# Putting the second layer's modulation products behind a later weight split, up to the first output projection

## The chip, the cores and the metric

The kernel runs on one core of a Trainium2 chip. The metric is the device time of one execution in microseconds (us). The engines are named as in the profile: PE (TensorE matmul), PEld (its weight loads), DVE (VectorE), ACT (ScalarE), POOL (GpSimd) and SP (SyncE, whose queue carries almost all of the loads).

## The reference, cut to what matters

Two residual layers of width 2048 work on 256 positions; a context of 256 positions feeds the first layer alone. Each layer begins with a modulation and ends with a gated residual and a layer norm:

```python
m = jax.nn.silu(cond) @ w_ada[i] + b_ada[i]      # 3 * 2048 outputs
sh, sc, gt = jnp.split(m, 3, axis=-1)
u = x * (1.0 + sc) + sh
y = mixer(u)          # layer 0: gated linear attention and a short convolution; layer 1: pooling
x = layer_norm(alpha * x + gt * y, ln_g[i], ln_b[i])
```

All is float32. `w_ada` is 2 x 2048 x 6144, so a third of it (one of `sh`, `sc`, `gt` of one layer) is 2048 x 2048, 16.8 MB. The two projections of layer 0 are `w_in_e` (2048 x 8224) and `w_out_e` (2048 x 2048), those of layer 1 `w_in_o` (2048 x 4096) and `w_out_o` (2048 x 2048).

## The kernel before

**Weight units.** Every large weight comes in units of 512 rows (four tiles of 128) by 512 columns, 1 MB each, by one DMA on SP's queue into a pool of four buffers (`raw`, L96). Each float32 unit is split into a rounded part and a remainder: ACT casts `wh` (L154), DVE subtracts to `wl` (L155), two instructions of each a unit. The parts lie in pools of four tiles each, which is two units. A product is three matmuls of 512 columns (`mm3`, L192 to L194). The list `specs` fixes the order of the units. `w_next` takes the next one; before that `w_ahead` loads up to two units further and splits one further. Below, units are counted along `specs` from 0.

**Modulation units.** The products of one row of activations with `w_ada` for layer 1's `sc` and `sh` and for both layers' `gt` are not made on PE. `ada_unit` (L505) loads 512 rows by 512 columns, 1 MB, into the same four `raw` buffers on the same queue, and `ada_accum` (L552) adds four tiles to an accumulator on DVE (L558 for the first, L560 for the rest). Four such units make a block of 512 columns. A block ends with small matmuls over the partitions: `adaS` (L581) for `sc` and `sh`, `gtb` (L547) for `gt`. Three generators run in the order `sc` of layer 1 (`c`), `gt` of layer 0 (`g`), `sh` of layer 1 (`h`), four blocks each, so 48 units. A fourth one makes layer 1's `gt` during layer 1.

**Pacing.** After each unit of a projection `tick` (L635) adds a credit and `pump_ada` (L497) takes that many steps of the generators. A step is one unit, or one end of a block. The credit of a tick is 3 during the six V units (`ADA_V`), 0.4 for the 16 units of q and of the first gate (`ADA_X`), 0.8 for the 32 units of the convolution branch (`ADA_C`), 1 during the output projection of layer 0 (`ADA_O`).

**The output projection of layer 0** (`ln_blocks`, L1102, called in L1196) takes 16 units, 76 to 91 along `specs`, in column blocks 0, 1, 2 and 3. Units 88 to 91 are block 3. Its matmuls run by row tile: row tile 0 with all four units, then row tile 1 with the same four. Ahead of block 3, `before()` calls `cols_ab` (L1166), which runs `pump_ada(1000)`: all that is left of the generators. Then come `A1` and `B1`, and `B1` (L1171) needs all of `sh`. `to_u1` (L1173) normalizes row tile 0 while PE works on row tile 1; it scales by `A1` and `B1` and gives the input of layer 1.

**Order on the engines.** The program text gives each instruction a place in a priority order; the framework orders each engine's instructions by that order and by when its own estimate finds them ready, and each engine then runs its list in order. Splits are raised by 300 places (`SPLIT_PRIO`). Loads keep their place in the text.

Of the kernel before, what the change touches and what calls it, by code (L numbers as in the profile page):

```python
# [9 lines left out]
F32 = mybir.dt.float32  # L10
# [3 lines left out]
ALU = mybir.AluOpType  # L14
# [48 lines left out]
def kernel(  # L63
# [24 lines left out]
    nc = tc.nc  # L88
    names = {}

    def nm(s):
        names[s] = names.get(s, 0) + 1
        return f"{s}_{names[s]}"
# [17 lines left out]
    def const(shape, dt, name):  # L111
        return cpool.tile(shape, dt, tag=name, name=name)
# [4 lines left out]
    def mp(shape, name="mp"):  # L117
        return mpp.tile(shape, F32, tag="mp", name=nm(name))
# [26 lines left out]
    def split_unit(r, nk, wide=False):  # L145
        parts = []
        for j in range(0, nk, 2):
            w = min(2, nk - j)
            if wide:
                h, l = slot([P, w, 512], F32R, "swh"), slot([P, w, 512], F32R, "swl")  # L150
            else:
                h = whp.tile([P, w, 512], F32R, tag="wh", name=nm("wh"))
                l = wlp.tile([P, w, 512], F32R, tag="wl", name=nm("wl"))
            nc.scalar.copy(h, r[:, j : j + w, :])  # L154
            nc.vector.tensor_tensor(out=l, in0=r[:, j : j + w, :], in1=h.bitcast(F32), op=ALU.subtract)  # L155
            for i in range(w):
                parts.append((h[:, i, :], l[:, i, :]))
        return parts
# [5 lines left out]
    wst = {"l": 0, "s": 0, "u": 0}  # L164
    wraws, wparts = {}, {}

    def w_ahead(nl, ns):
        top = len(specs)
        while wst["s"] < min(top, wst["u"] + ns):
            w_load(wst["s"] + 1)  # L170
            i = wst["s"]
            with prio(-SPLIT_PRIO if n0_done[0] else -SPLIT_PRIO0):
                wparts[i] = split_unit(wraws.pop(i), specs[i][2], i in wide)
            wst["s"] = i + 1
        w_load(min(top, wst["u"] + nl))

    def w_load(n):
        while wst["l"] < n:
            i = wst["l"]
            wraws[i] = load_unit(*specs[i])  # L180
            wst["l"] = i + 1
# [149 lines left out]
    k0 = 0  # L331
# [164 lines left out]

    def pump_ada(n):  # L497
        while n > 0 and ada_bg:
            try:
                next(ada_bg[0])  # L500
                n -= 1
            except StopIteration:
                ada_bg.pop(0)

    def ada_unit(layer, k0, n0):  # L505

        if not ADA_SLOT:
            r = load_unit(w_ada[layer], k0, 4, n0)
            return [r[:, j, :] for j in range(4)]
        q = {"s": nc.sync, "g": nc.gpsimd}[ADA_SLOT]  # L510
        parts = []
        for k in (k0, k0 + 2):
            r = slot([P, 2, 512], F32, "araw")
            q.dma_start(r, w_ada[layer][k * P : (k + 2) * P, n0 : n0 + 512].rearrange("(k p) n -> p k n", p=P))
            parts += [r[:, 0, :], r[:, 1, :]]
        return parts
# [16 lines left out]
    def ada_rows_gen(layer, dst, engs):  # L533

        for nb in range(4):
            if nb % 2 == 0:
                dst.append(slot([P, 2, 512], F32, "gt"))
            g = dst[nb // 2][:, nb % 2, :]
            n0 = 2 * D + nb * 512
            nc.gpsimd.dma_start(g, b_ada[layer : layer + 1, n0 : n0 + 512].to_broadcast([P, 512]))  # L540
            a = small([P, 512], "aacc1")
            for k0 in range(0, KT, 4):
                ada_accum(ada_unit(layer, k0, n0), k0, a, engs)
                if k0 == KT - 4:
                    yield
                    pb = mp([P, 512], "gtb")
                    nc.tensor.matmul(out=pb, lhsT=ones, rhs=a, start=True, stop=True)  # L547
                    nc.vector.tensor_tensor(out=g, in0=pb, in1=g, op=ALU.add)
                    gt_done.setdefault(id(dst), set()).add(nb)
                yield  # L550

    def ada_accum(r, k0, a, engs):  # L552
        e = engs[(k0 // 4) % len(engs)]
        with prio(ADA_PRIO):
            for j in range(4):
                sc = sil[:, k0 + j, 2:3]
                if k0 + j == 0:
                    e.tensor_scalar(out=a, in0=r[j], scalar1=sc, scalar2=None, op0=ALU.mult)  # L558
                else:
                    e.scalar_tensor_tensor(out=a, in0=r[j], scalar=sc, in1=a, op0=ALU.mult, op1=ALU.add)  # L560

    def ada_cols_gen(layer, n0, dst, bias, one, engs, on_pe=()):

        for nb in range(4):
            ns = slice(4 * nb, 4 * nb + 4)
            if nb in on_pe:
                hold = []
                for _ in ada_acc_gen(layer, n0 + nb * 512, hold):
                    if not hold:
                        yield  # L570
                add_bias(dst[:, ns], to_cols(hold[0], 512)[:, :, 0], bias[:, ns], one)
                yield
                continue
            a = small([P, 512], "aacc1")
            for k0 in range(0, KT, 4):
                ada_accum(ada_unit(layer, k0, n0 + nb * 512), k0, a, engs)
                yield
            yield
            pt = mp([P, 4], "adaS")
            for q in range(4):  # L580
                nc.tensor.matmul(out=pt[:, q : q + 1], lhsT=a[:, q * P : (q + 1) * P], rhs=ones[:, 0:1], start=True, stop=True)  # L581
            add_bias(dst[:, ns], pt, bias[:, ns], one)
# [9 lines left out]
    prev, k0 = None, 0  # L592
# [494 lines left out]
    for i in range(2):  # L1087
        n0 = i * 512
# [13 lines left out]
    def ln_blocks(src, order, getu, res, gt, budget, after, before=None, between=None, halves=False):  # L1102

        rt, accs, seen = {}, {}, {}

        def add(nb, m, cs=slice(0, 512)):
            if nb not in rt:
                rt[nb] = res(nb)
            while ada_bg and not (len(gt) > nb // 2 and nb in gt_done.get(id(gt), ())):
                pump_ada(1)  # L1110
            t = small([P, 512], "arow")[:, cs]
            nc.vector.tensor_tensor(out=t, in0=accs[nb][m + (cs.start > 0)][:, cs], in1=gt[nb // 2][:, nb % 2, cs], op=ALU.mult)
            r = rt[nb][:, m, cs]
            nc.vector.scalar_tensor_tensor(out=r, in0=r, scalar=ALPHA, in1=t, op0=ALU.mult, op1=ALU.add)
            parts = [r] if not (halves and m) or cs != slice(0, 512) else [r[:, 0:256], r[:, 256:512]]
            for v in parts:
                nc.vector.bn_stats(out=cst[m][:, seen_st[m], :], in_=v)
                seen_st[m] += 1

        def done(m, cs, end):  # L1120
            with prio(-LN_PRIO if m else 0):
                add(order[-1][0], m, cs)
                if not end:
                    return
                mv = small([P, 2], "mv")
                nc.vector.bn_aggr(out=mv, in_=cst[m][:, 0 : seen_st[m], :])
                after(m, rt, mv[:, 0:1], mv[:, 1:2])

        seen_st = [0, 0]
        for nb, qs in order[:-1]:  # L1130
            if 1 in qs:
                drain()
            if nb not in accs:
                accs[nb] = [acc_bank("oacc") for _ in range(2)]
                seen[nb] = 0
            gemm(src, nb * 512, qs, range(2), getu, accs[nb], first=seen[nb] == 0, last=seen[nb] + len(qs) == 4, budget=budget)
            seen[nb] += len(qs)
            if seen[nb] == 4:
                for m in range(2):
                    add(nb, m)  # L1140
        if before:
            before()
        nb, qs = order[-1]
        accs[nb] = [acc_bank("oacc") for _ in range(2)]
        gemm_by_tile([(src, nb * 512, qs, accs[nb], True)], getu, done, between=between, halves=halves)
        return rt
# [12 lines left out]
        return r  # L1159

    ada_credit[1] = ADA_O
    A1 = const([P, KT], F32, "A1")
    B1 = const([P, KT], F32, "B1")
    u1h, u1l, ufs, dms = [], [], [], []

    def cols_ab():  # L1166
        ln_exp_tables()
        pump_ada(1000)
        nc.vector.tensor_tensor(out=A1, in0=lngT, in1=scT1, op=ALU.mult)
        nc.vector.tensor_tensor(out=B1, in0=lnbT, in1=scT1, op=ALU.mult)  # L1170
        nc.vector.tensor_tensor(out=B1, in0=B1, in1=shT1, op=ALU.add)  # L1171

    def to_u1(m, rt, mean, var):  # L1173
        rstd = rsqrt_act(var)
        ms = slice(m * P, (m + 1) * P)
        for nb in range(4):
# [10 lines left out]
            for j in range(4):  # L1187
                kt = 4 * nb + j
                if j % 2 or (UF_ACT >> m) & 1:
                    nc.scalar.activation(uf[:, j, :], pt[:, j, :], AF.Identity, bias=B1[:, kt : kt + 1], scale=A1[:, kt : kt + 1])  # L1190
                else:
# [136 lines left out]
    for s in ODD:  # L1328
        g = int(s[1])
        if s == "g0":  # L1330
            accs = [acc_bank("xacc") for _ in range(2)]
            f = gate_evac(0)
# [81 lines left out]
```

## Time and profile before

| | |
|---|---|
| median of 3 runs | 997.5 us (997.06 to 998.74) |
| profiled execution | 1001.09 us |
| its span, first to last instruction | 999.3 us |
| mean granted TensorE clock | 0.983 of full speed |
| busy: PE / DVE / ACT | 959.7 / 801.0 / 469.4 us |
| DMA | 255.44 MB, mean 256 GB/s |

Matmuls overlap in the records, so PE counts as busy where one begins before the last has ended. Where PE is idle, work was late. Of DVE and of the DMA queues only that idle or busy time matters which PE has to wait for.

### The profile page before, as it was taken

The numbers are of one execution on the slowest core, as the hardware profiler recorded it, in microseconds if no ns is written. First come the engines' busy times: TensorE is split into PE (matmuls) and PEld (weight loads), VectorE is DVE, ScalarE is ACT, GpSimd is POOL, SyncE is SP. The second block draws the span as 40 slices with busy tenths as digits, with TensorE's granted clock in tenths as the row PEclk, the third lists the DMA queues.
The fourth block names the chain that finished last, engine by engine and source line by source line (L and its number), as shares of the span: only waits on it lengthen the run. The fifth ranks groups of instructions, "written<-read, shape, count | busy, mean of one in ns | idle before, by whom it ended". The sixth has DMA issues, their size and how long they took to land.

```text
span 999.3 us, 14376 instructions
## 1 busy us (share of the span) xinstructions
PE 959.7 (96%) x5684; PEld 767.0 (77%) x5684; DVE 801.0 (80%) x1143; ACT 469.4 (47%) x643; POOL 24.4 (2%) x56
## 2 busy tenths in 40 slices
PE   7899999999999999999999899999989999989995
PEld 5566766888878877887878788887778778768885
DVE  1456657999996999789999779897979997676676
ACT  2432224265774775245554344346644555444340
POOL 2000000000000000000000000000100001000000
PEclk9899999999999999999999999999999999999998
DMA  9988999577786677857776787994697999775532
GB/s 258 291 268 294 306 330 333 208 244 261 247 289 225 206 254 227 275 194 253 253 253 211 274 300 272 320 327 149 207 349 269 313 334 319 269 280 186 182 114 84
DMA packets 150371, 255.44 MB, mean 256 GB/s; under 512 B 5078, under 2 KB 46720, under 8 KB 150304
## 3 DMA queue, kind: packets, MB, share of 16 engines
q1 hardware_dynamic: 146592, 245.13, 72.8%
q0 software_dynamic: 2896, 8.72, 2.8%
q10 hardware_dynamic: 816, 0.68, 0.3%
q8 instruction: 44, 0.72, 0.3%
q14 instruction: 23, 0.19, 0.1%
HBM read 252.41 MB, written 2.10 MB: 255 GB/s over the span
## 4 chain that ended last, share of the span: by engine, by line
PE 56%; DVE 24%; DMA 14%; issue 3%; ACT 2%; SPq 1%; DVEq 0%; ACTq 0%
DMA raw<-in_w_ada_dram 11%; DVE wl L155 8%; PE oacc L193 6%; PE oacc L192 6%; PE oacc L194 6%; DVE aacc L560 6%; PE xacc L194 6%; PE xacc L192 6%; PE xacc L193 6%; DMA raw<-in_w_in_o_dram 3%; PE kacc L192 2%; PE ada L287 2%; PE kacc L193 2%; PE kacc L194 2%; ACT wh L154 1%
## 5 line engine op out<-in xcount | busy, mean ns | idle before, releaser
L154 ACT CAST wh<-raw 128x1024 fp32r<-128x1024 f32 (+1 forms) x250 | 257.3, 1044 | 256.7 <-PE xacc L194 86.0
L155 DVE TENSOR_TENSOR wl<-raw,wh 128x1024 fp32r<-128x1024 f32 (+1 forms) x250 | 297.8, 1210 | 50.2 <-ACT wh L154 48.3
L560 DVE SCALAR_TENSOR_TENSOR aacc<-raw,sil,aacc 128x512 f32<-128x512 f32 x240 | 178.8, 747 | 31.2 <-DMA raw<-in_w_ada_dram 27.8
L192 PE MATMUL xacc<-wh,uxh 128*128 128x512 f32 x384 | 154.1, 401 | 0.0
L193 PE MATMUL xacc<-wl,uxh 128*128 128x512 f32 x384 | 151.4, 394 | 0.9 <-DVE wl L155 0.9
L194 PE MATMUL xacc<-wh,uxl 128*128 128x512 f32 x384 | 151.6, 395 | 0.0
L193 PEld LDWEIGHTS xacc<-wl,uxh 128*128 128x128 f32 x384 | 72.8, 189 | 17.5 <-DVE wl L155 1.8
L192 PEld LDWEIGHTS xacc<-wh,uxh 128*128 128x128 f32 x384 | 72.8, 190 | 15.6 <-issue 0.5
L194 PEld LDWEIGHTS xacc<-wh,uxl 128*128 128x128 f32 x384 | 72.6, 189 | 15.6 <-issue 0.2
L452 DVE TENSOR_TENSOR knat<-kacc,knat 128x512 f32<-128x512 f32 x64 | 42.9, 685 | 32.1 <-PE kacc L194 31.8
L300 ACT COPY arow<-ada 128x256 f32<-128x256 f32 (+1 forms) x9 | 3.1, 349 | 93.2 <-PE ada L287 93.2
L192 PE MATMUL xacc<-wh,u1h 128*128 128x512 f32 x112 | 45.2, 403 | 0.8 <-ACT u1h L1193 0.8
L192 PE MATMUL oacc<-wh,y1h 128*128 128x512 f32 (+1 forms) x120 | 45.5, 379 | 0.0
L194 PE MATMUL oacc<-wh,y1l 128*128 128x512 f32 (+1 forms) x120 | 45.0, 375 | 0.0
L193 PE MATMUL oacc<-wl,y1h 128*128 128x512 f32 (+1 forms) x120 | 45.0, 375 | 0.0
L193 PE MATMUL xacc<-wl,u1h 128*128 128x512 f32 x112 | 44.6, 398 | 0.4 <-DVE wl L155 0.4
L194 PE MATMUL xacc<-wh,u1l 128*128 128x512 f32 x112 | 44.2, 395 | 0.0
L287 PE MATMUL ada<-raw,sil 128*32 128x256 f32 (+1 forms) x576 | 33.9, 367 | 7.8 <-DMA raw<-in_w_ada_dram 7.7
L287 PEld LDWEIGHTS ada<-raw,sil 128*32 128x32 f32 x576 | 15.7, 110 | 23.7 <-issue 9.4
L1254 PE MATMUL xacc<-wh,dm 128*128 128x512 f32 x64 | 26.2, 410 | 2.7 <-ACT wh L154 2.7
L192 PE MATMUL kacc<-wh,uxh 128*128 128x512 f32 x64 | 26.8, 419 | 0.0
L193 PE MATMUL kacc<-wl,uxh 128*128 128x512 f32 x64 | 26.0, 407 | 0.0
(342 smaller groups left out, 1874.9 us busy)
## 6 DMA issues: line engine op xcount, KB each, us to landing
raw<-in_w_ada_dram SPq DMA_DIRECT2D x96, 1024.0 KB, 6.4
raw<-in_w_in_e_dram SPq DMA_DIRECT2D x54, 1024.0 KB, 5.7
raw<-in_w_in_o_dram SPq DMA_DIRECT2D x32, 1024.0 KB, 7.1
raw<-in_w_out_e_dram SPq DMA_DIRECT2D x16, 1024.0 KB, 6.4
raw<-in_w_out_o_dram SPq DMA_DIRECT2D x16, 1024.0 KB, 5.1
raw<-in_w_in_e_dram SPq DMA_DIRECT2D x18, 512.0 KB, 6.3
raw<-in_w_pool_dram SPq DMA_DIRECT2D x4, 1024.0 KB, 7.7
gt<-in_b_ada_dram POOLq DMA_DIRECT2D x8, 256.0 KB, 3.9
```

The source lines that it names most:

```text
L154: nc.scalar.copy(h, r[:, j : j + w, :])
L155: nc.vector.tensor_tensor(out=l, in0=r[:, j : j + w, :], in1=h.bitcast(F32), op=ALU.subtract)
L192: nc.tensor.matmul(out=acc, lhsT=uh, rhs=wh, start=start, stop=False)
L193: nc.tensor.matmul(out=acc, lhsT=uh, rhs=wl, start=False, stop=False)
L194: nc.tensor.matmul(out=acc, lhsT=ul, rhs=wh, start=False, stop=stop)
L287: ins = nc.tensor.matmul(out=ps[32 * g : 32 * g + 32, :], lhsT=sil[:, kt, 2 - 2 * half : 34 - 2 * half], rhs=r[:, j, :], start=half == 0 a ...
L300: arow_ins.append(nc.scalar.copy(a[:, :nw], ps))
L452: nc.vector.tensor_tensor(out=dst, in0=acc, in1=dst, op=ALU.add)
L560: e.scalar_tensor_tensor(out=a, in0=r[j], scalar=sc, in1=a, op0=ALU.mult, op1=ALU.add)
L1254: nc.tensor.matmul(out=accs[0], lhsT=dh, rhs=wh, start=f, stop=False)
```

## The change

Up to layer 0's output projection, a modulation unit is still loaded at its step, but its four DVE instructions are put off. `put_off` files them with the number of weight units loaded so far. `w_ahead` issues them once it has split the first weight unit that was loaded after them, ordered behind that unit's last subtraction. At most two units are on file: a third pushes the first one out at once. A block's end waits for its products: as long as any are on file, the generator yields, and each such yield is a step that `pump_ada` counts. From the output projection on (`defer[0] = False`) products are issued directly, as before.

```diff
+            wl_ins.append(nc.vector.tensor_tensor(out=l, in0=r[:, j : j + w, :], in1=h.bitcast(F32), op=ALU.subtract))
...
+    def put_off(f):
+        if not defer[0]:
+            f()
+            return
+        while len(pend) >= 2:
+            pend.pop(0)[1]()
+        pend.append((wst["l"], f))
+
+    def pend_all():
+        while pend:
+            pend.pop(0)[1]()
...
             wst["s"] = i + 1
+            while pend and pend[0][0] <= i:
+                with tc.issue_after(wl_ins[-1].ins):
+                    pend.pop(0)[1]()
...
     def pump_ada(n):
         while n > 0 and ada_bg:
+            if n >= 500:
+                pend_all()
...
-                ada_accum(ada_unit(layer, k0, n0), k0, a, engs)
+                put_off(lambda r=ada_unit(layer, k0, n0), k0=k0, a=a: ada_accum(r, k0, a, engs))
                 if k0 == KT - 4:
                     yield
+                    while pend:
+                        yield
...
-                ada_accum(ada_unit(layer, k0, n0 + nb * 512), k0, a, engs)
+                put_off(lambda r=ada_unit(layer, k0, n0 + nb * 512), k0=k0, a=a: ada_accum(r, k0, a, engs))
+                yield
+            while pend:
                 yield
             yield
...
             while ada_bg and not (len(gt) > nb // 2 and nb in gt_done.get(id(gt), ())):
+                pend_all()
                 pump_ada(1)
...
     ada_credit[1] = ADA_O
+    defer[0] = False
+    pend_all()
```

## Rows read from the trace of the kernel before

**Rows 1.** Busy time over the span (page, part 1)

```profile
PE 959.7 (96%) x5684; PEld 767.0 (77%) x5684; DVE 801.0 (80%) x1143; ACT 469.4 (47%) x643; POOL 24.4 (2%) x56
```

**Rows 2.** By stretch: length, busy PE, PEld, DVE, ACT, POOL; clock, DMA share, GB/s

```profile
182.00:274.00 92.00, 92.00 (x432) 76.18 (x431) 85.62 (x136) 53.90 (x82) 0.51 (x5) 1.00 0.69 240
274.00:322.00 48.00, 45.96 (x271) 37.17 (x270) 39.90 (x54) 31.83 (x45) 1.41 (x5) 1.00 0.79 271
322.00:372.00 50.00, 50.00 (x459) 40.18 (x458) 49.98 (x63) 36.51 (x37) 0.00 (x0) 1.00 0.71 232
372.00:466.00 94.00, 92.60 (x683) 75.56 (x682) 81.83 (x117) 46.53 (x64) 1.06 (x2) 1.00 0.71 234
466.00:560.00 94.00, 93.94 (x756) 76.78 (x754) 91.33 (x123) 44.59 (x59) 1.40 (x2) 1.00 0.72 240
560.00:595.00 35.00, 32.04 (x138) 26.19 (x136) 24.30 (x45) 15.67 (x22) 1.50 (x3) 0.90 0.78 278
595.00:646.00 51.00, 51.00 (x242) 42.55 (x241) 46.55 (x63) 21.57 (x24) 0.00 (x0) 1.00 0.87 308
646.00:671.40 25.40, 25.40 (x118) 21.09 (x117) 25.04 (x31) 12.12 (x12) 0.00 (x0) 1.00 0.88 304
```

**Rows 3.** PE's waits from 182 to 600: us in total, times, longest

```profile
PE yT L1000 <- DVE y L992: 3.0, 1, 3.0
...
PE xacc L193 <- DVE wl L155: 0.9, 2, 0.6
```

**Rows 4.** PE and DVE in order of time around 569: start, us, [idle before]

```profile
569.25 0.75 DVE L560 SCALAR_TENSOR_TENSOR aacc<-raw,sil,aacc 128x512 f32<-128x512 f32 x1 [3.35 <-DMA raw<-in_w_ada_dram]
569.92 1.26 DVE L992 SCALAR_TENSOR_TENSOR y<-po,rsy,gs 128x256 f32<-128x256 f32 x3
...
570.55 1.09 PE L1000 MATMUL yT<-ident,y 128*128 128x128 f32 x4 [2.96 <-DVE y L992]
...
571.86 0.63 PE L193 MATMUL xacc<-wl,uxh 128*128 128x512 f32 x1
572.29 0.63 PE L194 MATMUL xacc<-wh,uxl 128*128 128x512 f32 x1
```

**Rows 5.** Line L560 alone from 182 to 274: busy (x instructions), clock, DMA

```profile
182.00:274.00 92.00, 39.43 (x53) 1.00 0.69 240
```

**Rows 6.** SP's waits before a load, over the span

```profile
SPq L140 <- DVE aacc L560: 139.4, 57, 8.7
```

**Rows 7.** SP's loads in order of time, from 645

```profile
645.95 0.37 SPq L140 DMA_DIRECT2D raw<-in_w_ada_dram  x1
646.61 16.39 SPq L140 DMA_DIRECT2D raw<-in_w_out_e_dram  x5
```

**Rows 8.** A stretch of steady loads, columns as in rows 2

```profile
100.00:180.00 80.00, 78.69 (x559) 56.31 (x558) 53.52 (x89) 23.36 (x41) 0.41 (x2) 1.00 0.99 320
```

**Rows 9.** DMA rate in slices of 2 us, 720 to 800

```profile
GB/s 372 326 376 264 288 325 399 386 386 388 378 376 334 368 251 363 406 381 384 351 305 132 369 38 51 287 200 261 300 350 387 295 226 140 394 298 407 373 354 193
```

**Rows 10.** DVE in order of time: one unit's four products in one piece

```profile
623.55 3.11 DVE L560 SCALAR_TENSOR_TENSOR aacc<-raw,sil,aacc 128x512 f32<-128x512 f32 x4
```

**Rows 11.** DVE's groups from 646 to 672: count, busy us, mean ns

```profile
L155 DVE TENSOR_TENSOR wl<-raw,wh 128x1024 fp32r<-128x1024 f32 x8 | 9.6, 1219 | 0.4 <-ACT wh L154 0.4
L560 DVE SCALAR_TENSOR_TENSOR aacc<-raw,sil,aacc 128x512 f32<-128x512 f32 x9 | 6.7, 744 | 0.0
```

**Rows 12.** PE and DVE in order of time, last block of the output projection

```profile
671.54 0.39 PE L192 MATMUL oacc<-swh,yah 128*128 128x512 f32 x1
...
676.98 0.39 PE L192 MATMUL oacc<-wh,ybh 128*128 128x512 f32 x1
...
685.99 0.68 DVE L1194 TENSOR_TENSOR u1l<-uf,u1h 128x512 fp32r<-128x512 f32 x1
...
690.10 0.39 PE L192 MATMUL xacc<-wh,u1h 128*128 128x512 f32 x1
```

**Rows 13.** ACT's half of a split (page, part 5)

```profile
L154 ACT CAST wh<-raw 128x1024 fp32r<-128x1024 f32 (+1 forms) x250 | 257.3, 1044 | 256.7 <-PE xacc L194 86.0
```

More of the change, by code (lines that the diff above doesn't have):

```diff
@@ L154, in split_unit @@
             nc.scalar.copy(h, r[:, j : j + w, :])
-            nc.vector.tensor_tensor(out=l, in0=r[:, j : j + w, :], in1=h.bitcast(F32), op=ALU.subtract)
+            wl_ins.append(nc.vector.tensor_tensor(out=l, in0=r[:, j : j + w, :], in1=h.bitcast(F32), op=ALU.subtract))
             for i in range(w):
@@ L165 @@
     wraws, wparts = {}, {}
+    pend, wl_ins = [], []
+    defer = [True]
+    def put_off(f):
[8 more added lines that the diff above has]
+            pend.pop(0)[1]()
     def w_ahead(nl, ns):
```

## The prediction

> **What bounds the kernel now.** I read the page's first part, then busy time by stretch. PE is busy for 959.7 of 999.3 us [rows 1], and the stretches say where it is not. From 182 to 595, which is V to the end of the convolution branch and so the whole reach of the putting off, idle PE sums to 0 + 2.04 + 0 + 1.40 + 0.06 + 2.96 = 6.5 us; from 595 to 671.4, in the output projection, it is 0 [rows 2]. So PE is the bound. DVE is nearly one too (91.33 of 94 from 466 to 560, 25.04 of 25.4 from 646 to 671.4 [rows 2]), but its work pays only where PE waits for it.
>
> Then PE's waits from 182 to 600. The longest is 3.0 us at 570 for `y`; two for `wl` make 0.9 [rows 3]. The order of time shows the first one's cause: DVE waits 3.35 us, in front of `y`, for the load of a modulation unit [rows 4]. The gap costs more than itself. PE's granted clock over the 35 us from 560 is 0.90 [rows 2], so 0.10 x 35 / 0.5 = 7 us of it ran at the lower level, 1.2 GHz, with matmuls 0.43 us apart [rows 4] where 24 of them from 671.54 to 676.98 are 0.227 apart [rows 12]. That is 7 x (1 - 0.227 / 0.43) = 3.3 us lost.
>
> **Part 1: products behind a later split.** The DVE instructions stay the same, 4 a unit, 3.11 us in one piece [rows 10]; only their place changes. A unit put off after unit u waits for the split of u+3, made two units later, so its load has landed by then and DVE no longer waits for it. Best case: 3.0 for the gap, 3.3 for its clock and 0.9 for the two late `wl`, 7.2 us gained. Against it, a unit on file keeps its buffer longer, and at most two of four are so kept. SP already waits 57 times, 139.4 us in all and at most 8.7, for products to free a buffer [rows 6]. PE feels none of it, as the loads run two units ahead, about 11 us at 24 x 0.227 = 5.4 a unit. I bound the loss at one such wait laid bare, 8.7 us. I take a gain of 5, near the best case because the one large gap has the very cause that is removed.
>
> **Part 2: the steps.** This decides. While a block waits for products on file, the generator yields, and `pump_ada` counts each yield as a step. Steps before the output projection: 6 x 3 + 16 x 0.4 + 32 x 0.8 = 50. Before, a block takes 5 steps (4 units and its end), so 50 steps are 10 blocks, 40 units. The trace agrees for the first stretch: 53 instructions of L560 from 182 to 274, with 4 of L558 14 units of the V stage's 15 [rows 5].
>
> After, in V: tick 1 files units 1 to 3 (the third pushes out the first). Tick 2 files unit 4 and spends two steps waiting, tick 3 all three: unit 4 leaves the file only with the split before tick 4. Tick 4 makes the end and two units of the next block, tick 5 two units and a wait, tick 6 three waits. So V's 18 steps give 8 units, 1 end and 9 waits, where before they gave 15 units and 3 ends. The 16 slow units lose 1 more step and the convolution's 32 lose 2, by the same walk. That is 12 lost, 38 left: 7 blocks and 3 units, 31 units instead of 40.
>
> What does V gain from the 7 units it sheds? Nothing: PE is busy for 92.00 of its 92.00 us [rows 2].
>
> **Part 3: where the 9 units go.** 17 are left for the output projection, where 8 were. Its first 12 ticks make 12 steps: 9 units and 3 ends. The other 8 units go to `pump_ada(1000)` in one piece, right in front of block 3. In text order the loads are then: unit 87, one modulation unit, 88, another, 89, the eight, 90, 91. On SP's queue, in order and through four buffers, 90 is the 14th load counted from 87. Before, 87 is issued at 646.61 and all of 87 to 91 within 16.39 us [rows 7].
>
> A load's price in a steady stretch: 1.049 MB at 320 GB/s and a DMA share of 0.99 [rows 8] is 3.28 us. 14 x 3.28 = 45.9, so unit 90 lands at 692.5. DVE gives about the same: from 646 to 671.4 it works 25.04 us [rows 2], of which products are 6.7 and the split of 91 2.4 [rows 11], so 16 remain; ten units add 10 x 3.11 = 31.1 [rows 10]; 646 + 47.1 = 693.1. With the first cast (1.04 [rows 13]) and subtraction (1.22 [rows 11]) PE can begin unit 90 at 694.8. Before, it began at 671.54 [rows 12].
>
> Row tile 1's share of 88 and 89 (5.4 us) can be pulled into the gap. But row tile 0 must end before `to_u1`: 694.8, unit 91 split 3.28 later at 698.1, its 12 matmuls until 700.8. From that end to layer 1's first input tile took 676.98 to 686.67, 9.7 us [rows 12]. So layer 1 starts at 710.5 instead of 690.10 [rows 12]: 20.4 us late. PE then stood idle for over 10 us; the fall to the lower clock adds between 0 and the 3.3 above, and I take 2. Loss: 22.4.
>
> Bounds of it. Low: each load at the 386 GB/s that several slices reach [rows 9], 2.72 us. Then 90 lands at 684.7, row tile 0 ends at 692.4, layer 1 starts at 702.1: 12.0 and, with part of the clock, 13.6. High: two more loads in front (one issued at 645.95 [rows 7] still in flight, one late), 6.6 us: 29.
>
> By the Trainium skill (DMA: Bandwidth & Descriptors, Specifications) the fabric's ceiling is 435 GB/s. By that, as an estimate, a load would take 2.41 us and the loss would be about 8 us instead of 22; no steady stretch of this trace comes near it, the best here is 320.
>
> **Sum.** -5 + 22.4 = +17. The profiled execution took 1001.1, so the same one would take 1018; it is 3.6 above the median of the runs, and on the median 997.5 + 17 = 1014.5, rounded to 1014. Layer 1's own modulation is not put off, and its loads shift with the rest: nothing there.
>
> **The rivals.**
>
> *Faster.* The same gain of up to 7.2 with no burst. The place is the eight units in front of block 3, the point their number. With n of them unit 90 lands at 646.61 + (6 + n) x 3.28. For n = 4 that is 679.4, layer 1 starts 7.3 late and the gain is used up; from 3 down the change wins, at n = 0 with 990.5. For it: that DVE wait at 569 is real. Against it: n = 8 follows from the walk, whatever the engines do. Nor can rate save it, since breaking even at n = 8 needs 14 loads in 33 us, 444 GB/s, and the best slice shows 407 [rows 9]. 7 in 100.
>
> The Trainium skill (DMA: Bandwidth & Descriptors, Rules for kernel authors) speaks for this rival: issue a DMA early and wait for it late. The change does that with every product it puts off; the wait of 3.35 us [rows 4] is what the rule would remove.
>
> *No change.* Gain and burst cancel, within 2 us of 997.5 (0.2%, about what a measurement of this kernel can tell): it needs the low price of loads, the whole gain and block 3's row tile 1 pulled forward without loss. 5 in 100.
>
> *The burst is mostly hidden.* Loads at 386 GB/s and the whole gain of 7: +2 to +8, 1000 to 1005. 11 in 100.
>
> *The buffers starve PE.* Two of four on file, in the stage where DVE is busiest, lay bare one wait of 2 to 3 us in each of seven blocks, some with a slower clock behind it: 10 to 20 us on top of the burst, above 1028. Against it: PE's idle time there is almost nil, and loads have 11 us of lead. 7 in 100.
>
> **How the numbers follow.** My forecast has 70 in 100 and lies between +8 and +30. Slower by over 0.2% is that and the last two rivals, 0.88; same 0.05; faster 0.07. The range leaves out the faster rival, no change and the upper part of starvation: 1003 to 1028.
>
> **What would show it.** In the changed kernel's trace: some 8 units of L560's counterpart from 182 to 274 instead of 14; the wait for `y` at about 569 gone, with the clock at full there; eight loads from `w_ada` in a row on SP right before the last two of `w_out_e`; PE idle for 10 to 20 us just before the first matmul on `swh`, `B1` later than 690; the rest shifted as it is. I am wrong if PE begins unit 90 within 5 us of the end of 89, if PE waits for `wl` before the output projection, or if the gap at 569 only moves.

## The result, and the profile after

The changed kernel takes 1032.7 us (median of 4 runs, 1027.1 to 1035.6), the kernel before beside it 997.8 (997.06 to 998.74): a ratio of 1.0348, 95% interval 1.0316 to 1.0380. The prediction's 1014 was right in its sign and too low by 18.7 us; its range ended at 1028. The profiled execution took 1035.6 us with a span of 1033.8, where before had 999.3.

Busy time over the span, against [rows 1]:

```profile
PE 967.7 (94%) x5684; PEld 775.0 (75%) x5684; DVE 803.8 (78%) x1143; ACT 472.2 (46%) x645; POOL 24.4 (2%) x56
```

The work is the same: 5684 matmuls and 1143 DVE instructions on both sides, DVE's busy time 2.8 us apart. What changed is where it stands. I cut both traces at the first matmul of V (`vacc`), of the output projection (`oacc`), of layer 1 (on `u1h`) and on `dm`; us:

| from, to | before | after | difference |
|---|---|---|---|
| start, V | 191.77 | 188.18 | -3.6 |
| V, output projection | 404.36 | 398.40 | -6.0 |
| output projection, layer 1 | 93.97 | 128.10 | **+34.1** |
| layer 1, `dm` | 14.43 | 21.13 | +6.7 |
| `dm`, end of span | 294.79 | 298.02 | +3.2 |

The first row is no effect of the change, which touches nothing ahead of V: the profiles of the twelve experiments below, whose programs don't differ up to V either, begin it anywhere from 187.71 to 191.53. So the way from V to the projection gained 6.0 us, the output projection lost 34.1, and layer 1 another 9.9. Each number is from one profile. The six kernels that have the changed program up to the projection gain 4.4 to 6.8 us there. From `dm` on the program is the same in all fourteen profiles, and it takes 292.2 to 298.4 us, so the last row's 3.2 are not shown to be an effect; the 6.7 above them are.

Busy time by stretch of the changed kernel, against [rows 2], and its output projection as a whole in the last line (columns as there):

```profile
182.00:274.00 92.00, 91.97 (x422) 75.60 (x421) 71.11 (x109) 58.68 (x90) 0.61 (x6) 1.00 0.52 174
...
466.00:560.00 94.00, 90.41 (x729) 72.83 (x728) 86.71 (x118) 43.38 (x62) 3.23 (x5) 0.98 0.71 235
560.00:595.00 35.00, 34.56 (x164) 28.21 (x163) 26.72 (x45) 18.59 (x22) 0.72 (x1) 1.00 0.81 277
595.00:646.00 51.00, 50.39 (x222) 40.58 (x221) 50.15 (x69) 19.28 (x22) 0.00 (x0) 1.00 0.89 311
...
586.58:714.68 128.10, 102.03 (x447) 83.17 (x446) 118.23 (x170) 39.27 (x49) 0.00 (x0) 0.88 0.89 308
```

The same output projection in the kernel before:

```profile
596.13:690.10 93.97, 93.79 (x442) 77.78 (x440) 84.21 (x114) 43.02 (x56) 0.00 (x0) 1.00 0.84 297
```

Before, PE is busy for all but 0.2 us of this stage and DVE for 84.2. After, DVE works 118.2 us, 34.0 more, and the stage is 34.1 longer. Much of that is arithmetic: nine more units at 3.11 us [rows 10] are 28.0, and 84.2 + 28.0 = 112.2 is more than the 94.0 that the stage took. The products alone (PE, PEld, DVE on the accumulators `aacc`; after, then before):

```profile
586.58:714.68 128.10, 6.66 (x34) 5.95 (x34) 55.56 (x77) 0.88 0.89 308
596.13:690.10 93.97, 2.86 (x24) 3.01 (x24) 23.34 (x32) 1.00 0.84 297
```

76 products begin in the stage instead of 32 (x77 counts one that begins just before it), which is eleven units more and not nine: two of the 31 units loaded ahead of the projection are multiplied only in it.

DVE is not the only full resource. 128.10 us at 308 GB/s are 39.5 MB, against 27.9 MB before. At the 320 GB/s of [rows 8] that is, as an estimate, 123 us of loads (no hard bound: from 672.75 to 700.06 they ran at 338). Which of the two binds is not settled by these rows.

Where the units went shows in line L583 alone (L560 before), from 182 to 274, against [rows 5]:

```profile
182.00:274.00 92.00, 21.38 (x29) 1.00 0.52 174
```

29 products instead of 53: about 8 units instead of 14, as the walk through the steps said. SP's loads in order of time, against [rows 7]:

```profile
643.72 0.37 SPq L140 DMA_DIRECT2D raw<-in_w_ada_dram  x1
644.38 0.37 SPq L140 DMA_DIRECT2D raw<-in_w_out_e_dram  x1
649.77 0.37 SPq L140 DMA_DIRECT2D raw<-in_w_ada_dram  x1
651.81 0.37 SPq L140 DMA_DIRECT2D raw<-in_w_out_e_dram  x1
657.39 24.00 SPq L140 DMA_DIRECT2D raw<-in_w_ada_dram  x8
681.69 4.92 SPq L140 DMA_DIRECT2D raw<-in_w_out_e_dram  x2
```

These are the eight loads in one piece ahead of units 90 and 91, in the order that was predicted. PE's waits from 560 to 745 (in all, times, longest; "issue" means that the engine waited for nothing that the profile shows):

```profile
PE adaS L606 <- DVE aacc L583: 21.7, 2, 12.1
PE xacc L1282 <- ACT dm L1238: 4.9, 1, 4.9
PE xT L1213 <- issue: 3.2, 1, 3.2
```

PE in order of time around them, against [rows 12] (start, length, [idle before]):

```profile
668.64 0.40 PE L213 MATMUL oacc<-wh,ybl 128*128 128x512 f32 x1
681.14 1.84 PE L606 MATMUL adaS<-ones,aacc 128*128 128x1 f32 x8 [12.11 <-DVE aacc L583]
692.57 1.87 PE L606 MATMUL adaS<-ones,aacc 128*128 128x1 f32 x8 [9.59 <-DVE aacc L583]
694.29 1.20 PE L211 MATMUL oacc<-swh,yah 128*128 128x512 f32 x2
...
699.13 0.63 PE L212 MATMUL oacc<-swl,yah 128*128 128x512 f32 x1
699.56 0.63 PE L213 MATMUL oacc<-swh,yal 128*128 128x512 f32 x1
...
702.07 0.39 PE L211 MATMUL oacc<-swh,yah 128*128 128x512 f32 x1
702.29 0.39 PE L212 MATMUL oacc<-swl,yah 128*128 128x512 f32 x1
...
707.73 0.39 PE L213 MATMUL oacc<-swh,yal 128*128 128x512 f32 x1
711.35 2.79 PE L1213 MATMUL xT<-ident,xr 128*128 128x128 f32 x12 [3.23 <-issue]
714.68 0.80 PE L211 MATMUL xacc<-wh,u1h 128*128 128x512 f32 x1 [0.54 <-ACT u1h L1221]
```

From 668.64 to 694.29 PE does nothing but two block ends (`adaS`), and each waits for the last product of its block. In the same time DVE makes those products back to back:

```profile
667.88 9.41 DVE L583 SCALAR_TENSOR_TENSOR aacc<-raw,sil,aacc 128x512 f32<-128x512 f32 x12
...
683.10 9.41 DVE L583 SCALAR_TENSOR_TENSOR aacc<-raw,sil,aacc 128x512 f32<-128x512 f32 x12
692.43 2.35 DVE L155 TENSOR_TENSOR swl<-raw,swh 128x1024 fp32r<-128x1024 f32 x2
```

The last line is the split of unit 90, behind all of them. Its load was late as well; ACT's cast begins only when that has landed:

```profile
690.11 1.99 ACT L154 CAST swh<-raw 128x1024 fp32r<-128x1024 f32 x2 [29.74 <-DMA raw<-in_w_out_e_dram]
```

The last rows of the PE list show a second cost. Row tile 1's share of units 88 and 89 was pulled ahead of the gap, so between the end of row tile 1 (707.73) and layer 1's first matmul (714.68) only the 2.79 us of `xT` stand. Before, layer 1 followed the last `oacc` without a gap, because row tile 1's 13 us of matmuls covered the layer norm of row tile 0.

### The profile page after: what moved, and what is told of

It is laid out like the page before. It is cut to its first block, busy times and chain, and to the rows that moved or that the text cites. A ratio compares the mean times of both kernels' runs of the same rounds, so it can differ in the third digit from the quotient of the medians.

```text
span 1033.8 us, 14377 instructions
## 1 busy us (share of the span) xinstructions
PE 967.7 (94%) x5684; PEld 775.0 (75%) x5684; DVE 803.8 (78%) x1143; ACT 472.2 (46%) x645; POOL 24.4 (2%) x56
## 4 chain that ended last, share of the span: by engine, by line
PE 66%; DVE 16%; DMA 12%; issue 3%; ACT 3%; ACTq 0%; DVEq 0%; SPq 0%
DMA raw<-in_w_ada_dram 8%; PE xacc L211 7%; PE xacc L213 7%; PE xacc L212 7%; DVE wl L155 6%; PE oacc L211 5%; PE oacc L212 5%; PE oacc L213 5%; DVE aacc L583 5%; PE kacc L211 2%; DMA raw<-in_w_in_e_dram 2%; PE ada L306 2%; PE kacc L212 2%; PE kacc L213 2%; PE vacc L211 2%
## 5 line engine op out<-in xcount | busy, mean ns | idle before, releaser
L583 DVE SCALAR_TENSOR_TENSOR aacc<-raw,sil,aacc 128x512 f32<-128x512 f32 x240 | 179.1, 750 | 17.8 <-DMA raw<-in_w_ada_dram 14.1
L212 PEld LDWEIGHTS xacc<-wl,uxh 128*128 128x128 f32 x384 | 72.4, 189 | 14.8 <-issue 0.2
L471 DVE TENSOR_TENSOR knat<-kacc,knat 128x512 f32<-128x512 f32 x64 | 43.0, 687 | 32.4 <-PE kacc L213 32.1
L211 PE MATMUL xacc<-wh,u1h 128*128 128x512 f32 x112 | 45.9, 409 | 0.5 <-ACT u1h L1221 0.5
L154 ACT CAST swh<-raw 128x1024 fp32r<-128x1024 f32 x16 | 16.2, 1047 | 32.2 <-DMA raw<-in_w_out_e_dram 30.4
L606 PE MATMUL adaS<-ones,aacc 128*128 128x1 f32 x64 | 9.4, 268 | 21.7 <-DVE aacc L583 21.7
```

Source lines behind the costliest of these rows:

```text
L211: nc.tensor.matmul(out=acc, lhsT=uh, rhs=wh, start=start, stop=False)
L212: nc.tensor.matmul(out=acc, lhsT=uh, rhs=wl, start=False, stop=False)
L471: nc.vector.tensor_tensor(out=dst, in0=acc, in1=dst, op=ALU.add)
```

## The experiments

For each profile I give three differences to before in us, cut as in the table above: V to projection, projection to layer 1, layer 1 to the end. The changed kernel has -6.0, +34.1, +9.9.

**The steps kept.** A wait for products does not use up a step.

```diff
                     while pend:
-                        yield
+                        yield "wait"
...
-                next(ada_bg[0])
+                if next(ada_bg[0]) == "wait":
+                    return n
...
-        pump_ada(int(ada_credit[0]))
-        ada_credit[0] -= int(ada_credit[0])
+        k = int(ada_credit[0])
+        ada_credit[0] -= k - pump_ada(k)
```

> The changed kernel, but a generator that waits for its products ends the tick and keeps its credit, so no step is lost: 40 units lie ahead of the output projection again and none is left for the piece in front of block 3. Theory S (the lost steps cost the time): 986 to 998 us, since the first matmul of the output projection came 9.6 us earlier in the changed kernel and that is kept, and PE waits less than 3 us before layer 1's first input. Theory P (putting off itself costs, by buffers held and by another order): 1020 us or more.

1009.6 us, ratio 1.0143 (1.0097 to 1.0190); +7.6, +1.7, -0.8. With 40 units ahead, the loss in the output projection is gone, so the lost steps of Part 2 are what costs the projection its time, as Part 3 says. But V to projection now costs more, and the time lies between the two that were expected. Its waits of PE from 182 to 600:

```profile
PE nT L738 <- ACT qn L845: 4.2, 2, 4.0
PE xacc L211 <- ACT wh L154: 4.1, 4, 1.7
PE xacc L212 <- DVE wl L155: 3.0, 4, 1.0
```

The longest stand around 271, 288 and 292, and the clock of the stretch 260 to 310 is 0.90. Saved credit came out in bursts there (SP issues four units in a row at 249.93), so this kernel does not price the putting off by itself.

**Lost steps alone.** The timetable of the change, with each product issued directly.

```diff
-        pend.append((wst["l"], f))
+        f()
+        pend.append((wst["l"], lambda: None))
```

> The changed kernel with each unit's products issued directly, as before the change, but with the same waits counted as steps: the timetable of the changed kernel (31 units ahead of the output projection, 17 in it, eight of them in one piece), and nothing put off. Theory S: 1025 to 1040 us, like the changed kernel or a little slower, as the gap at 569 us may be back. Theory P: 996 to 1003 us, like the kernel before.

1026.2 us, ratio 1.0308 (1.0266 to 1.0350); -10.8, +32.4, +3.5. The putting off is gone and nearly the whole loss stays. So does the relief ahead of the projection, which is even larger: fewer units are enough to remove the gap at 569, without any putting off. From 560 to 745 PE waits for

```profile
PE adaS L607 <- DVE aacc L584: 11.0, 2, 10.0
PE oacc L212 <- ACT swh L154: 7.8, 1, 7.8
PE xacc L1283 <- ACT dm L1239: 5.0, 1, 5.0
PE xT L1214 <- issue: 3.2, 1, 3.2
```

**Putting off alone.** Before's timetable: at a block's end the products on file are issued at once instead of waited for.

```diff
                     while pend:
-                        yield
+                    pend_all()
...
-            while pend:
-                yield
-            yield
+            pend_all()
+            yield
```

(In the first place the loop goes with its `yield`.)

> The changed kernel in which a block's end issues what is on file instead of waiting for it: the timetable of loads and steps of the kernel before, unit by unit, with the products put off inside each block. Theory A (putting off costs nothing or gains, and the 12 us of the run with kept credit came from its four units in one tick): 988 to 999 us. Theory B (putting off itself costs, by buffers held and by block ends that PE reaches before their products): 1002 to 1012 us.

998.1 us (10 runs), ratio 0.9993 (0.9972 to 1.0013); -3.3, +3.6, +1.3. Putting the products off is worth nothing that can be measured. The gap at 569 is gone here too, with as many units as before, so the putting off removes it as Part 1 said. But the 3.3 us gained are lost again in the next stage: DVE has 27.8 us of products there instead of 23.3, since some were put off across its start. (The products still on file at a block's end are issued there, so the run prices a somewhat shorter delay than that of the changed kernel.) The Trainium skill (DMA: Bandwidth & Descriptors, Rules for kernel authors) would have a DMA issued early and waited for late; this kernel does that for the products it puts off. The wait for the load at 569 goes, as the rule has it, but the ratio is 0.9993.

**All 17 units spread.** Twice the rate during the projection, so that no piece is left.

```diff
-ADA_O = 1
+ADA_O = 2
```

> The changed kernel with a credit of 2 instead of 1 in the output projection: the same 17 units in it, spread over its ticks, none in one piece. If the number of units in that stage costs (DMA and DVE are full there): 1015 to 1030 us, with PE waiting for splits all over the stage instead of in front of block 3. If the one piece costs, through PE's queue waiting at the matmuls that end the two blocks: 995 to 1010 us.

1030.4 us, ratio 1.0356 (1.0313 to 1.0400); -5.9, +29.3, +8.4. No piece, and nearly the same loss. PE now waits in many places (8.4 us in four for `wh`, 7.8 in six for `wl`), and DVE is busy for most of the stage:

```profile
586.84:710.08 123.24, 105.67 (x447) 83.06 (x446) 115.51 (x161) 38.66 (x47) 0.00 (x0) 0.93 0.91 320
```

So the place of the eight is not all: nine more units cost nearly as much at either rate that was tried. The loads run at 320 GB/s here, the rate of [rows 8].

**The piece alone.** The kernel before with no credit in the projection: its own eight units, all in front of block 3.

```diff
-ADA_O = 1
+ADA_O = 0
```

> The kernel before with no credit during the output projection: 40 modulation units ahead of it and 8 in it, as before, but all eight in one piece in front of block 3, and none beside blocks 0 to 2. The number is that of before, the place that of the change. If the place costs by itself (the piece's loads and products stand in front of block 3, PE waits for the last block end, and the layer norm's chain behind row tile 0 has lost the matmuls that cover it), PE waits for adaS for 8 to 20 us, layer 1 starts 10 to 25 us late against the start of the projection, and the time is 1008 to 1027. If the nine additional units are the cost, some 3.1 us of DVE and 3.3 us of loading each wherever they stand, then with eight units nothing is added: DVE and the loads have room in blocks 0 to 2 in place of it, and the time is within 4 us of the kernel before.

1020.6 us, ratio 1.0240 (1.0182 to 1.0299); -0.5, +20.4, +1.9. Its code up to the projection is that of before, and so is that time within 0.5 us. The stage as a whole:

```profile
593.35:707.70 114.35, 101.15 (x438) 82.59 (x436) 88.40 (x123) 40.16 (x49) 0.00 (x0) 0.90 0.71 244
```

PE's longest waits from 560 to 745 are 6.1 us for the split of unit 90, 5.0 for `dm` and 3.2 each for `xT` and `y`; at `adaS` it waits 2.5, not the 8 to 20 expected. SP's loads in order of time:

```profile
646.82 26.52 SPq L140 DMA_DIRECT2D raw<-in_w_ada_dram  x8
674.96 4.00 SPq L140 DMA_DIRECT2D raw<-in_w_out_e_dram  x2
```

DVE has only 88.4 us of work in 114.4 here. What it lacks in blocks 0 to 2 it cannot do earlier, since the program issues these loads and products only at the piece. The place by itself costs 20.4, the number by itself 29.3 and both together 34.1. They do not add; presumably both act through the time at which DVE and the queue are through with what stands ahead of block 3, which no run shows by itself.

**Loads first.** Units 88 to 91 are loaded and split ahead of the piece.

```diff
         ln_exp_tables()
+        w_ahead(4, 4)
         pump_ada(1000)
```

> The changed kernel with units 88 to 91 loaded and split ahead of the piece of eight. If PE lacks units 90 and 91 there (the prediction's step): at least 10 us less than the changed kernel, 1015 to 1023 us. If PE stands at the matmuls that end the blocks, which lie ahead of block 3 in its order and wait for the products: within 5 us of it, 1026 to 1036 us, with the two waits of 12 and 10 us still there.

1027.1 us, ratio 1.0308 (1.0252 to 1.0364); -6.0, +33.6, +5.0. PE is through with block 3 at 682 and then waits for the two block ends, which DVE now reaches later, 694 and 708 instead of 681 and 693:

```profile
694.33 1.84 PE L606 MATMUL adaS<-ones,aacc 128*128 128x1 f32 x8 [12.08 <-DVE aacc L583]
708.09 1.87 PE L606 MATMUL adaS<-ones,aacc 128*128 128x1 f32 x8 [11.92 <-DVE aacc L583]
```

Layer 1 needs the last of them. The 45.9 us of loads in front of unit 90 were therefore not the only chain: with unit 90 out of the way, the piece's products hold layer 1 as late.

**The last two blocks on PE.** The same loads, but PE makes the products of `sh`'s blocks 2 and 3 instead of DVE; then the same with the loads first.

```diff
-ADA_PE = ((), ())
+ADA_PE = ((), (2, 3))
```

> The changed kernel with the products of the last two blocks of sh, the eight units in one piece, made by PE matmuls instead of DVE; their loads stay as and where they are. If DVE's work is what the piece costs (34 us more of it between the start of the output projection and layer 1, of which these eight units are 25): the two waits of 12 and 10 us shrink and the time falls by 10 us or more, to 1005 to 1022 us. If the loads cost: 1025 us or more, and PE waits for the eight loads or for units 90 and 91 instead.

> The same with units 88 to 91 loaded and split ahead of the eight loads. If DVE alone was the cost, it is within 3 us of the run without that order. If the loads are the next bound behind DVE, PE gets block 3 earlier but still waits for the last of the eight before layer 1: 3 to 8 us less than without it, 1000 to 1015 us.

The first: 1029.4 us, ratio 1.0289 (1.0236 to 1.0341); -5.6, +31.8, +7.5. DVE is down to 96.2 us in the stage, and nearly the whole loss stays, so DVE's busy time is not its only cause. Units 90 and 91 are issued at 682.38, behind the eight. Both together: 1022.0 us, ratio 1.0239 (1.0205 to 1.0273); -6.8, +28.7, +1.5. Here PE's waits from 660 to 712 begin with

```profile
PE xT L1214 <- issue: 11.1, 2, 9.9
```

That is the layer norm's chain, which block 3's matmuls no longer cover. It is also held up by the piece. DVE makes one instruction of it at 684.22, and the profile puts the wait before the next down to the last block end (`adaT` on PE, behind the last of the eight loads):

```profile
693.77 0.69 DVE L1138 TENSOR_TENSOR arow<-oacc,gt 128x512 f32<-128x512 f32 x1 [8.87 <-PE adaT L322]
```

The stage as a whole:

```profile
586.49:709.11 122.62, 108.61 (x519) 82.86 (x518) 96.98 (x140) 42.11 (x55) 0.00 (x0) 0.93 0.91 322
```

DVE is far from full, but the same 39.5 MB are loaded at 322 GB/s, and PE, which now makes the products, is busy for 14.8 us more than before. Loads, DVE's products and the layer norm's chain lie close behind one another; these runs do not separate what each would cost alone.

**More units beside q.** 36 units ahead instead of 31, twelve left, four of them in the piece.

```diff
-ADA_X = 0.4
+ADA_X = 1.0
```

> The changed kernel with a credit of 1 instead of 0.4 for the 16 units of q and the first gate: by the walk 36 units lie ahead of the output projection (31 in the changed kernel, 40 before), so 12 in it, of which three or four in one piece. If each unit beyond the eight of before costs that stage its DVE products and its load, 3.1 to 3.3 us: four units, about 13 us there instead of 34, 1002 to 1012 us in all. If only a piece of eight costs, through the wait behind it: within 4 us of the kernel before.

1030.3 us, ratio 1.0324 (1.0290 to 1.0357); +3.7, +22.6, +9.0. The five units cost the stretch up to the projection its relief of 6.0 and 3.7 more. Four units above before's eight still cost 22.6, 5.6 each, so no fixed price for a unit holds. What stays whole is the end: PE waits 6.2 us for the split of unit 90, 3.2 for `xT` and 5.0 for `dm`. Why the end costs so much with a piece of four is not settled.

**The clock kept up.** Eight matmuls of no use, 256 columns each, behind every load of the piece.

```diff
+                rr = ada_unit(layer, k0, n0 + nb * 512)
+                put_off(lambda r=rr, k0=k0, a=a: ada_accum(r, k0, a, engs))
+                if dummies[0]:
+                    idle = mp([P, 256], "idle")
+                    for _ in range(dummies[0]):
+                        nc.tensor.matmul(out=idle, lhsT=rr[3][:, 0:P], rhs=zero, start=True, stop=True)
...
+        dummies[0] = 8
         pump_ada(1000)
```

> The changed kernel with eight matmuls without use (256 columns of zeros, their result is read by nothing) behind each load of the piece of eight, so that PE works during its wait. If the lower clock after the wait is a good part of the loss there and in the first blocks of layer 1: the granted clock stays at full from 670 to 740 and the time falls by 6 to 11 us, to 1022 to 1027 us. If PE's wait alone counts: within 3 us of the changed kernel, whatever the clock.

1030.2 us, ratio 1.0334 (1.0300 to 1.0368); -4.4, +31.3, +6.4. From 670 to 733 the granted clock was

```profile
670.00:733.00 63.00, 58.82 (x288) 48.88 (x286) 53.90 (x87) 26.04 (x48) 0.00 (x0) 1.00 0.69 237
```

In the changed kernel it was 0.50, the level of 1.2 GHz, from 672.75 to 700.06. The stage became 2.8 us shorter and the whole no faster beyond the intervals. But the added matmuls cost time themselves: DVE's last product ends at 694.74, and PE is through with them only at 699.9. Up to unit 90's first matmul, and from there to layer 1:

```profile
590.06:700.57 110.51, 109.89 (x510) 91.64 (x509) 104.61 (x142) 31.99 (x35) 0.00 (x0) 1.00 0.89 307
700.57:715.37 14.80, 14.32 (x72) 11.42 (x71) 10.92 (x19) 6.79 (x12) 0.00 (x0) 1.00 1.01 374
```

In the changed kernel the two parts take 107.71 and 20.39. So 2.8 us were lost in the first and 5.6 won in the second: about 5.6 is what the clock costs from unit 90 to layer 1, and most of the 34.1 is not the clock.

**Other timetables of the kernel before.** Fewer units in V and more beside the convolution; then the reverse.

```diff
-ADA_V = 3
+ADA_V = 1.5
-ADA_C = 0.8
+ADA_C = 1.1
```

> The kernel before with a credit of 1.5 in V instead of 3 and of 1.1 instead of 0.8 in the convolution branch: still 50 steps ahead of the output projection, nothing put off, but V's units fewer. If the 11 us that the lost steps gave ahead of the output projection came from the relief of V and of the q units: 985 to 993 us. If they came from fewer units altogether, or the convolution branch (DVE busy 91 of 94 us) can't take more: 996 to 1006 us.

1017.5 us, ratio 1.0183 (1.0151 to 1.0215); +19.8, +1.8, -1.3. The convolution's stage can't take V's units either: PE waits 5.4 us for `y`, 3.4 for `wl`, 2.9 for `gtb`.

```diff
-ADA_V = 3
+ADA_V = 3.5
-ADA_C = 0.8
+ADA_C = 0.7
```

> The kernel before with a credit of 3.5 instead of 3 in V and of 0.7 instead of 0.8 in the convolution branch: 40 units ahead of the output projection as before, three more of them in V, nothing put off. If DVE in the convolution branch is what makes units dear there (nine units moved into it from V cost 18 us): the gap at 569 us goes and the time falls to 988 to 994 us. If V has no room either: 996 to 1003 us.

996.4 us (10 runs), ratio 0.9997 (0.9981 to 1.0012). The gap at 569 is gone here as well, but nothing is gained that can be measured. No kernel tried was faster than before.

## Why the prediction was wrong

**Part 1, the putting off: forecast -5; by itself it is worth nothing that can be measured.** V to projection did fall by 6.0, close to the forecast, and the wait for `y` fell from 3.0 [rows 3] to 0.4 with the clock at 1.00 from 560. But that agreement is luck: the lost steps alone gave 10.8 there without any putting off, and the putting off alone ended at 0.9993. The gap itself was read rightly, since putting off alone removes it. What failed is that the gain lasts: with before's timetable the 3.3 us came back in the output projection, where the products now stood. In the changed kernel a new wait of 2.7 us for `gtb`, up to 525.64, took part of the gain back. The bound on starved buffers held: SP's longest wait for a product fell from 8.7 us [rows 6] to 6.3 (for L581; 5.8 for L583).

**Part 2, the steps: right.** 31 units ahead instead of 40; 8 in V; 17 left, 8 in one piece; the order of the loads. Only its last sentence is off: the shed units do help, not in V but up to the projection, by 10.8 us without the putting off.

**Part 3: the right place, the size too small.** Forecast 20.4 and 2 for the clock, measured 34.1. Its own steps, moved by the 9.55 us by which the projection began earlier:

| step | forecast, moved | measured | later by |
|---|---|---|---|
| PE begins unit 90 | 685.25 | 694.29 | 9.0 |
| row tile 0 ends | 691.25 | 702.95 | 2.7 more |
| layer 1 starts | 700.95 | 714.68 | 2.0 more |

(Row tile 0's end is taken at the DVE instruction that it releases, and each row's delay is counted from the row above.) The second row is the clock, which I had put at 2: for 5.7 us after unit 90's start, at a granted clock of 0.50, the matmuls stand 0.43 us apart, and 0.227 after that. The first step failed in DVE's sum, "of which products are 6.7 [...] so 16 remain; ten units add": 16 us of other work and ten units, 47.1 us from 646. From 636.45, the same point, to 692.50 the trace has 56.05 us, 51.95 of them busy, and these groups lead:

```profile
L583 DVE SCALAR_TENSOR_TENSOR aacc<-raw,sil,aacc 128x512 f32<-128x512 f32 x45 | 33.3, 750 | 0.9
L155 DVE TENSOR_TENSOR wl<-raw,wh 128x1024 fp32r<-128x1024 f32 x9 | 10.6, 1222 | 0.0
```

With the three products of L581 that is 48, twelve units and not ten. The two more were issued on SP but not yet multiplied at that point (627.62 and 634.34). The kernel before has two as well at 646 (638.09 and 645.95): they are the 6.7 us of products that my sum struck out. With them it gives 53.8 us. The busy time came out 4.9 us above the 47.1, and the other 4.1 of the 9.0 are DVE's idle time, 2.2 of it spent waiting for `adaS` of the block just ended. The sum over the loads was too short as well: moved by 9.55, unit 90 was to land at 682.95, and its cast begins on its landing at 690.11. The loads did not run at the steady rate: from 586 to 690 SP waits 17 times, 46.4 us in all, for products of L583 to free a buffer. PE's wait is shown at the block ends, which stand ahead of unit 90 in its order, and not at unit 90, as in my sum.

The 20.4 that I gave is also what the piece alone costs, but in the sum only: there PE begins unit 90 14.3 us later than before, and I had 23.3. What I left out is the number. Nine more units fill DVE (115.5 of 123.2 us) and the loads even when they are spread (+29.3). I had noted DVE as "nearly" a bound without adding 28.0 us to its 84.2, and had summed the loads from unit 87 on only.

**Layer 1, "nothing there": measured +9.9, of which 6.7 stand out of the scatter.** Row tile 0's layer norm lost its cover, so layer 1 begins both row tiles late and at the lower clock; from the last `oacc` to the first matmul on `dm` it takes 27.7 us at a mean clock of 0.79 instead of 14.3 at 1.00. Half of that difference lies ahead of layer 1's first matmul and is in the 34.1. With the clock kept up, 5.3 of the 6.7 stay, so most of it is not the clock. PE waits 4.9 us for `dm` there; before, its longest wait from 690 to 740 was 2.7, for `wh`.

The rivals: faster, no change and mostly hidden are out by the interval. The buffers that starve PE would have given a time above 1028 as well, but PE's waits from 182 to 600 sum to 4.5 us. So the time lay beyond my range for another reason than the rival named.

## What to carry to other kernels

When a stage takes work over from another, add its price to each engine's busy time in that stage first, and compare with the stage's length: here 84.2 + 28.0 against 94.0 told that no placing of the units could save it. Do the same for the loads: 27.9 MB and nine units of 1.049 MB are 37.4 MB, 117 us at 320 GB/s. Sums that fit are not enough, though: the piece alone fits both and cost 20.4 us. An "empty" turn that a pacing loop counts is a change of the timetable, and here the timetable alone cost 3.1% where putting off alone cost nothing. A gap that goes away says little: the one at 569 went with fewer units, with products put off and with three units moved to V, and none of these kernels is faster.

## What was not expected of the hardware

PE stood 12.1 and 9.6 us at eight small matmuls (`adaS`, 1.84 us) while the split of unit 90 was queued on DVE behind the same products. It looks as if those matmuls held the stage, but with block 3 ahead of them the stage was only 0.5 us shorter. And 27.3 us at half the clock (1.2 GHz), of which PE was busy for 9.3, cost about 5.6 us up to layer 1: with the clock kept at full by useless matmuls the stage was 2.8 us shorter, and the whole run not measurably.
